# Norm factors along the rows: column sums by a product with ones, the root by Ln, Exp and one Newton step

## The chip, the cores and the metric

The kernel runs on one core of one Trainium2 chip. The metric is the device time of one execution in microseconds (us); the time before is the median of three runs.

## The reference, cut to what matters

One input of 512 tokens with 1024 features goes through three layers, all in float32. The first layer mixes three branches (gated linear attention, sliding-window attention, pooling) and has a feed-forward network with a short convolution; the second has attention with a forget gate ("fox") and a feed-forward network; the third has attention over a latent ("MLA") and a feed-forward network. Between all of them stand norms over the features of a token:

```python
def rmsnorm(x, gain):
    xf = x.astype(jnp.float32)
    var = jnp.mean(xf * xf, axis=-1, keepdims=True)
    return (xf * lax.rsqrt(var + RMS_EPS) * gain.astype(jnp.float32)).astype(x.dtype)
# first_block:  x = x + rmsnorm(merged @ w_out, norm_mix_post);  x = x + rmsnorm(f, norm_ffn_post)
# every layer:  h = rmsnorm(x, ...) ahead of each projection;  the last: rmsnorm_2(x, final_norm)
```

What concerns the change is the factor `1 / sqrt(mean of squares + eps)`, one number for each of the 512 tokens.

## The kernel before, in words

All activations are held transposed: the features lie in the 128 partitions (eight tiles of 128 features, `xk(0)` to `xk(7)`), the 512 tokens along the rows. A matmul with a weight tile gives 128 output features by 512 tokens in one PSUM bank. Each float32 product is made of three fp32r matmuls (`mm3`, high and low parts), so TensorE (PE) has some 10,500 matmuls. The weights come in 360 chunks of eight 128x128 tiles in the order of `tfk_plan`; each chunk is loaded by SP, cast to its high part by ScalarE (ACT, L277) and gets its low part from VectorE (DVE, L278), two chunks ahead of use (`take`, `_split`).

The order on PE is written out: the program runs `proj` calls in sequence, and small generators ("tasks") are stepped between them by `tick` when a modelled PE clock has passed their due time, which the constants `LAG` set. The order on the other engines comes from a scheduler with priorities, and each engine runs its instructions in that order, waiting for what is not ready.

A norm factor is needed along the rows, in all partitions, since it multiplies tiles of features by tokens. The squares are added over the eight tiles in `acc` (128x512), by GpSimd (POOL) and for the last tile by DVE (L507). Then:

- `tok_sums` multiplies each 128 tokens of `acc` with one column of ones: the sums come out by token, one number in each partition, and there are four pairs of weight load and matmul for 512 tokens, each in two passes.
- `_rsqrt` makes the root on DVE of these few numbers: an estimate from the bits and three Newton steps, some 12 tiny instructions.
- `bcast` puts the factors on a diagonal (DVE, L490) and multiplies it with ones on PE, so that they stand along the rows in a PSUM bank (`bc`); `stats_task` copies it to SBUF (L518) as `rsb`.

Who uses this: `stats` (task `stats_task`), for the norms ahead of projections, eight times: `mix_pre`, `ffn_pre`, `fox_norm`, `ffn_a`, `kv_in`, the two latents of MLA (`dkv`, `dq`), `ffn_b`; `chain` in `post_norm`, for the two norms behind the mixer (`wout`) and the first feed-forward network (`down0`), each in two halves of 256 tokens; `finish`, the last norm, in two halves, at the very end. `mix_pre` and `fox_norm` also need the factor by token (`rst`), since there values are projected with tokens in the partitions. In `chain` each half is followed by eight products on DVE (L962), eight additions to x on POOL (L963) and the splitting of x for the next projection (`x_ready`: L420 on ACT, L421 on DVE, the squares L504, L507), while PE is at the second half of the projection or at the first half of the next layer. In `finish` eight products (L1007) are followed by the stores of the output.

Of the kernel before, what the change touches and what calls it, by code (L numbers as in the profile page):

```python
# [7 lines left out]
F32 = mybir.dt.float32  # L8
F32R = mybir.dt.float32r
I32 = mybir.dt.int32  # L10
AF = mybir.ActivationFunctionType
# [184 lines left out]
class Net:  # L196
    def __init__(self, ctx, tc, xin, wall, par, cst, msk, nar, out, dbg=None):
# [15 lines left out]
        self.ones = self.cpool.tile([P, P], F32, name="ones")  # L213
        nc.gpsimd.memset(self.ones, 1.0)
        self.lows = [self.cpool.tile([P, 2, T], F32R, name=f"lows{i}") for i in range(2)]
        self.ident = self.c("ident", 128)
# [267 lines left out]
    def bcast(self, rs):  # L484
# [10 lines left out]
        return pb  # L495

    def tok_sums(self, acc, out, ms=range(4)):
        for i, m in enumerate(ms):
            self.mm(out[:, i:i + 1], acc[:, m * P:(m + 1) * P], self.ones[:, 0:1], True, True)
# [9 lines left out]

    def stats_task(self, acc, d, fut, lag):  # L510
        nc = self.nc
        pt = self.ps("tok")
        self.tok_sums(acc, pt)
        rs = self.rsqrt(pt[:, 0:4], 1.0 / d, 4)
        yield LAG[lag]
        pb = self.bcast(rs)
        rsb = self.pool.tile([P, T], F32, tag="rsb", name="rsb", bufs=2)
        nc.scalar.copy(out=rsb, in_=pb)  # L518
        fut.set((rsb, rs))

    def stats(self, acc, d, lag="sums", lag2="rsqrt"):
        fut = Fut(self)
        self.tasks.insert(0, [self.stats_task(acc, d, fut, lag2), self.clock + LAG[lag]])
        return fut
# [9 lines left out]
    def x_ready(self, k, cols=ALL):  # L534
# [20 lines left out]
        if self.next_gain == "final":  # L555
            nc.scalar.activation(out=x, in_=x, func=AF.Copy, scale=self.p("final", k))
        elif k == 7 and cols != HALVES[0]:
            self.rs = self.stats(self.acc, 1024, "sums_first" if self.next_gain == "mix_pre" else "sums" if cols == ALL else "sums_late")

# [376 lines left out]
    def post_norm(self, name, xs, gain, nxt, group, whole):  # L936
# [15 lines left out]
        def chain(h):  # L952
            cols = HALVES[h]
            pt = self.ps("tok")
            self.tok_sums(acc, pt, (2 * h, 2 * h + 1))
            rs = self.rsqrt(pt[:, 0:2], 1.0 / 1024, 2)
            yield LAG["chain"]
            pb = self.bcast(rs)
            for t in range(8):
                yt = y[t // 2][:, t % 2, cols]  # L960
                x = self.xk(t)[:, cols]
                v.tensor_tensor(out=yt, in0=yt, in1=pb[:, 0:256], op=ALU.mult)  # L962
                nc.gpsimd.tensor_tensor(out=x, in0=x, in1=yt, op=ALU.add)  # L963
                self.x_ready(t, cols)

        self.x_start(nxt)
# [6 lines left out]
    def residual(self, name, xs, nxt, k0=0, group=0):  # L973
# [3 lines left out]
        for t in range(8):  # L977
            x = self.xk(t)
            if nxt == "final" and t == 7:
                for h, cols in enumerate(HALVES):  # L980
                    ps = self.proj(name, t, xs, k0, None, cols)
                    with self.tc.high_priority(offset=2000):
# [3 lines left out]
                        self.nc.scalar.activation(out=x[:, cols], in_=x[:, cols], func=AF.Copy, scale=self.p("final", t))  # L986
                    self.tasks.insert(0, [self.finish(h, sq), self.clock + LAG["last"]])
                continue
# [5 lines left out]
    def finish(self, h, sq):  # L994

        nc, v = self.nc, self.nc.vector
        cols = HALVES[h]
        pt = self.ps("tok")
        for i, m in enumerate((2 * h, 2 * h + 1)):
            for a in (self.acc, sq):  # L1000
                self.mm(pt[:, i:i + 1], a[:, m * P:(m + 1) * P], self.ones[:, 0:1], a is self.acc, a is sq)
        rs = self.rsqrt(pt[:, 0:2], 1.0 / 1024, 2)
        yield LAG["last_rsqrt"]
        pb = self.bcast(rs)
        for k in range(8):
            x = self.xk(k)[:, cols]
            v.tensor_tensor(out=x, in0=x, in1=pb[:, 0:256], op=ALU.mult)  # L1007
            if k % 2:
                nc.sync.dma_start(out=self.out[:, k - 1:k + 1, cols], in_=self.x[k // 2][:, :, cols])
# [420 lines left out]
```

## Time and profile before

| | us |
|---|---|
| median of three runs | 2225.93 (2223.95 to 2228.35) |
| the profiled execution, its own time | 2225.05 |
| its span in the trace | 2223.3 |
| PE busy | 2165.1 (97%) |
| DVE busy | 1423.7 (64%) |
| ACT busy | 1022.2 (46%) |
| POOL busy | 282.1 (13%) |
| mean granted PE clock | 0.991 |

The span is what the trace covers; the profiled execution's own time is 1.75 us longer. "Busy" counts the time in which an engine has at least one instruction under way. A row of a timeline gives start, duration, engine, line, operation, tiles, and in brackets how long the engine had been idle before it and what ended that.

### The profile page before, as it was taken

The numbers are of one execution on the slowest core, as the hardware profiler recorded it, in microseconds if no ns is written. First come the engines' busy times: TensorE is split into PE (matmuls) and PEld (weight loads), VectorE is DVE, ScalarE is ACT, GpSimd is POOL, SyncE is SP. The second block draws the span as 40 slices with busy tenths as digits, with TensorE's granted clock in tenths as the row PEclk, the third lists the DMA queues.
The fourth block names the chain that finished last, engine by engine and source line by source line (L and its number), as shares of the span: only waits on it lengthen the run. The fifth ranks groups of instructions, "written<-read, shape, count | busy, mean of one in ns | idle before, by whom it ended". The sixth has DMA issues, their size and how long they took to land.

```text
span 2223.3 us, 27520 instructions
## 1 busy us (share of the span) xinstructions
PE 2165.1 (97%) x10536; PEld 1822.0 (82%) x10536; DVE 1423.7 (64%) x2372; ACT 1022.2 (46%) x1676; POOL 282.1 (13%) x242
## 2 busy tenths in 40 slices
PE   8989999999999998999999999999999999999998
PEld 6777788898888897888888888887888888888887
DVE  6897545578777238787677774357646567777524
ACT  4454232445444235676544443245755655444322
POOL 5221000040000004464200000102100101000010
PEclk9999999999999999999999999999999999999999
DMA  4211333322233344433233323332122223333332
GB/s 163 76 39 48 95 95 95 114 89 73 96 101 97 95 126 133 134 105 97 84 93 97 95 95 98 101 100 76 48 76 67 67 60 98 99 95 95 96 103 96
DMA packets 61956, 206.29 MB, mean 93 GB/s; under 512 B 7152, under 2 KB 9584, under 8 KB 61824
## 3 DMA queue, kind: packets, MB, share of 16 engines
q1 hardware_dynamic: 61392, 203.74, 29.4%
q8 instruction: 83, 1.36, 0.2%
q10 hardware_dynamic: 432, 0.79, 0.1%
q14 instruction: 49, 0.40, 0.1%
HBM read 197.65 MB, written 2.13 MB: 90 GB/s over the span
## 4 chain that ended last, share of the span: by engine, by line
PE 84%; DVE 9%; ACT 3%; issue 2%; DMA 1%; POOL 0%; SPq 0%; DVEq 0%; ACTq 0%; POOLq 0%
PE up L340 32%; PE down L340 15%; PE mout L340 4%; PE uq L340 3%; PE sc L340 2%; PE gate_a L340 2%; PE gate_b L340 2%; PE gate_c L340 2%; PE wout L340 2%; PE fout L340 2%; DVE lo L278 2%; DVE xs L421 1%; PE mpo L340 1%; PE dq L340 1%; PE fq L340 1%
## 5 line engine op out<-in xcount | busy, mean ns | idle before, releaser
L278 DVE TENSOR_TENSOR lo<-raw,hi 128x1024 fp32r<-128x1024 f32 (+1 forms) x348 | 438.1, 1259 | 318.0 <-ACT hi L277 313.6
L340 PE MATMUL up<-xs,hi 128*128 128x512 f32 x2016 | 621.8, 390 | 0.0
L277 ACT CAST hi<-raw 128x1024 fp32r<-128x1024 f32 (+1 forms) x348 | 365.2, 1049 | 554.2 <-PE down L340 170.5
L340 PEld LDWEIGHTS up<-xs,hi 128*128 128x128 f32 x2016 | 378.3, 188 | 78.9 <-issue 1.0
L340 PE MATMUL up<-xs,lo 128*128 128x512 f32 x1008 | 392.2, 389 | 0.0
L340 PE MATMUL down<-hl,hi 128*128 128x512 f32 (+1 forms) x1188 | 332.6, 366 | 0.0
L340 PEld LDWEIGHTS down<-hl,hi 128*128 128x128 f32 x1188 | 214.9, 189 | 36.2
L340 PEld LDWEIGHTS up<-xs,lo 128*128 128x128 f32 x1008 | 189.3, 188 | 39.6
L340 PE MATMUL down<-hl,lo 128*128 128x512 f32 (+1 forms) x594 | 217.1, 365 | 0.0
L507 POOL TENSOR_TENSOR acc<-acc,sq 128x256 f32<-128x256 f32 (+1 forms) x48 | 56.1, 1169 | 765.2 <-ACT sq L504 763.6
L1024 DVE TENSOR_TENSOR u<-up,rsb 128x512 f32<-128x512 f32 x132 | 90.1, 685 | 80.9 <-PE up L340 76.7
L1026 ACT ACTIVATE c<-u,par 128x512 f32<-128x512 f32 x132 | 107.0, 814 | 59.9 <-DVE u L1024 59.8
L340 PEld LDWEIGHTS down<-hl,lo 128*128 128x128 f32 x594 | 112.0, 189 | 18.0
L1027 DVE SCALAR_TENSOR_TENSOR c<-u,par,c 128x511 f32<-128x511 f32 x132 | 98.3, 746 | 23.8 <-ACT c L1026 23.7
L963 POOL TENSOR_TENSOR x<-x,yo 128x256 f32<-128x256 f32 x32 | 28.6, 930 | 633.3 <-DVE yo L962 633.3
L1028 DVE SCALAR_TENSOR_TENSOR c<-u,par,c 128x510 f32<-128x510 f32 x132 | 98.8, 749 | 4.0
L340 PE MATMUL uq<-hl,hi 128*128 128x512 f32 x288 | 89.5, 391 | 1.4 <-POOL hl L458 1.4
L457 ACT CAST hl<-c 128x512 fp32r<-128x512 f32 x66 | 40.7, 617 | 104.6 <-DVE c L1035 104.6
L340 PE MATMUL mout<-hl,hi 128*128 128x512 f32 x256 | 79.9, 393 | 0.0
L1033 ACT ACTIVATE c<-c 128x512 f32<-128x512 f32 x66 | 41.6, 630 | 70.4 <-DVE c L1028 70.3
L421 DVE SCALAR_TENSOR_TENSOR xs<-x,par,xs 128x512 fp32r<-128x512 f32 (+1 forms) x64 | 61.9, 1005 | 8.0 <-ACT xs L420 8.0
L340 PEld LDWEIGHTS uq<-hl,hi 128*128 128x128 f32 x288 | 53.9, 188 | 13.3 <-POOL hl L458 1.8
(398 smaller groups left out, 3933.9 us busy)
## 6 DMA issues: line engine op xcount, KB each, us to landing
raw<-in_wall_dram SPq DMA_DIRECT2D x359, 512.0 KB, 3.5
K<-KH SPq DMA_DIRECT2D x36, 128.0 KB, 2.3
bias<-cumd SPq DMA_DIRECT2D x16, 256.0 KB, 4.1
out_dram<-x SPq DMA_DIRECT2D x8, 256.0 KB, 2.3
x<-in_x_dram SPq DMA_DIRECT2D x7, 256.0 KB, 6.0
raw<-in_wall_dram SPq DMA_DIRECT2D x2, 256.0 KB, 3.9
early<-in_cst_dram SPq DMA_DIRECT2D x1, 512.0 KB, 6.5
msk<-in_msk_dram SPq DMA_DIRECT2D x1, 512.0 KB, 6.6
```

Source lines behind the costliest of these rows:

```text
L277: nc.scalar.copy(out=hi[:, c], in_=raw[:, c])
L278: nc.vector.tensor_tensor(out=lo[:, c], in0=raw[:, c], in1=hi[:, c].bitcast(F32), op=ALU.subtract)
L340: self.nc.tensor.matmul(out, lhsT=a, rhs=b, start=start, stop=stop)
L421: nc.vector.scalar_tensor_tensor(out=lo, in0=src, scalar=scale, in1=hi.bitcast(F32), op0=ALU.mult, op1=ALU.subtract)
L457: nc.scalar.copy(out=hi, in_=src)
L507: (eng or self.nc.vector).tensor_tensor(out=acc[:, cols], in0=acc[:, cols], in1=sq[:, cols], op=ALU.add)
L963: nc.gpsimd.tensor_tensor(out=x, in0=x, in1=yt, op=ALU.add)
L1024: v.tensor_tensor(out=u, in0=ps, in1=rsb, op=ALU.mult)
L1026: nc.scalar.activation(out=c, in_=u, func=AF.Identity, scale=self.p(conv, 88 + t), bias=self.p(conv, 132 + t))
L1027: v.scalar_tensor_tensor(out=c[:, 1:], in0=u[:, 0:T - 1], scalar=self.p(conv, 44 + t), in1=c[:, 1:], op0=ALU.mult, op1=ALU.add)
L1028: v.scalar_tensor_tensor(out=c[:, 2:], in0=u[:, 0:T - 2], scalar=self.p(conv, t), in1=c[:, 2:], op0=ALU.mult, op1=ALU.add)
L1033: nc.scalar.activation(out=g, in_=g, func=func)
```

## The change

The factors are now made along the rows. `all_sums` multiplies the whole 128x128 tile of ones with `acc`, so that each partition gets the sums of all tokens at once, in a PSUM bank. `row_factors` makes the root there, on 128x512 (or 128x256) elements: y = Exp(-0.5 Ln(s/d + eps)) on ACT, then one Newton step y (1.5 - 0.5 (s/d + eps) y^2), whose square is made on ACT and the rest on DVE. `stats` has a new argument `by_token`: `mix_pre` and `fox_norm` keep the old way; the six others, the four halves of `chain` and the two of `finish` take the new one. `stats_task` then has no second stage: the waiting time `rsqrt` and the product of `bcast` fall away. In `finish` the sum over `acc` is started at once and the last square added to it later.

```diff
+    def row_factors(self, sums, inv_d, out):
+        nc, v = self.nc, self.nc.vector
+        n = sums.shape[-1]
+        a, y, t = (self.t2(name=f"f{i}")[:, 0:n] for i in "ayt")
+        with self.tc.high_priority(offset=1000):
+            nc.scalar.activation(out=y, in_=sums, func=AF.Ln, scale=inv_d, bias=self.eps)
+            v.tensor_scalar(out=a, in0=sums, scalar1=-0.5 * inv_d, scalar2=-0.5 * EPS, op0=ALU.mult, op1=ALU.add)
+            nc.scalar.activation(out=y, in_=y, func=AF.Exp, scale=-0.5)
+            nc.scalar.activation(out=t, in_=y, func=AF.Square)
+            v.tensor_tensor(out=t, in0=a, in1=t, op=ALU.mult)
+            v.scalar_tensor_tensor(out=out, in0=t, scalar=1.5, in1=y, op0=ALU.add, op1=ALU.mult)
+        return out
+    def all_sums(self, accs, cols):
+        pt = self.ps("all")
+        n = cols.stop - cols.start
+        for i, a in enumerate(accs):
+            self.mm(pt[:, 0:n], self.ones, a[:, cols], i == 0, i == len(accs) - 1)
+        return pt[:, 0:n]
-    def stats_task(self, acc, d, fut, lag):
+    def stats_task(self, acc, d, fut, lag, by_token):
         nc = self.nc
+        if not by_token:
+            rsb = self.pool.tile([P, T], F32, tag="rsb", name="rsb", bufs=2)
+            fut.set((self.row_factors(self.all_sums([acc], ALL), 1.0 / d, rsb), None))
+            return
...
         def chain(h):
             cols = HALVES[h]
-            pt = self.ps("tok")
-            self.tok_sums(acc, pt, (2 * h, 2 * h + 1))
-            rs = self.rsqrt(pt[:, 0:2], 1.0 / 1024, 2)
-            yield LAG["chain"]
-            pb = self.bcast(rs)
+            rs = self.row_factors(self.all_sums([acc], cols), 1.0 / 1024, self.t2(name="rh")[:, 0:256])
             for t in range(8):
...
-                v.tensor_tensor(out=yt, in0=yt, in1=pb[:, 0:256], op=ALU.mult)
+                v.tensor_tensor(out=yt, in0=yt, in1=rs, op=ALU.mult)
...
-                    self.tasks.insert(0, [self.finish(h, sq), self.clock + LAG["last"]])
+                    self.tasks.insert(0, [self.finish(h, sq), self.clock])
...
-        pt = self.ps("tok")
-        for i, m in enumerate((2 * h, 2 * h + 1)):
-            for a in (self.acc, sq):
-                self.mm(pt[:, i:i + 1], a[:, m * P:(m + 1) * P], self.ones[:, 0:1], a is self.acc, a is sq)
-        rs = self.rsqrt(pt[:, 0:2], 1.0 / 1024, 2)
-        yield LAG["last_rsqrt"]
-        pb = self.bcast(rs)
+        pt = self.ps("all")[:, 0:256]
+        self.mm(pt, self.ones, self.acc[:, cols], True, False)
+        yield LAG["last"]
+        self.mm(pt, self.ones, sq[:, cols], False, True)
+        rs = self.row_factors(pt, 1.0 / 1024, self.t2(name="rh")[:, 0:256])
         for k in range(8):
             x = self.xk(k)[:, cols]
-            v.tensor_tensor(out=x, in0=x, in1=pb[:, 0:256], op=ALU.mult)
+            v.tensor_tensor(out=x, in0=x, in1=rs, op=ALU.mult)
```

## Rows read from the trace of the kernel before

**Rows 1.** The page: busy us, share of the span and instructions of each engine.

```profile
PE 2165.1 (97%) x10536; PEld 1822.0 (82%) x10536; DVE 1423.7 (64%) x2372; ACT 1022.2 (46%) x1676; POOL 282.1 (13%) x242
```

**Rows 2.** Waits of PE: total us, times, longest.

```profile
PE tok L340 <- DVE acc L507: 7.9, 4, 4.7
...
PE bc L340 <- DVE diag L490: 4.1, 3, 2.8
...
PE uq L340 <- POOL hl L458: 1.4, 1, 1.4
...
PE fv L340 <- DVE xs L421: 1.3, 2, 0.7
```

**Rows 3.** Timeline of PE at the token sums of `ffn_a`: start, us, operation.

```profile
1109.22 0.39 PE L340 MATMUL up<-xs,lo 128*128 128x512 f32 x1
1109.45 0.94 PE L340 MATMUL tok<-ones,acc 128*128 128x1 f32 x8
1110.26 0.72 PE L340 MATMUL up<-xs,hi 128*128 128x512 f32 x2
1110.82 0.40 PE L340 MATMUL up<-xs,lo 128*128 128x512 f32 x1
```

**Rows 4.** The same view at the broadcast product of `ffn_pre`.

```profile
506.13 1.02 PE L340 MATMUL bc<-diag,ones 128*128 128x512 f32 x2
506.59 0.80 PE L340 MATMUL up<-xs,khi 128*128 128x256 f32 x2
507.23 0.28 PE L340 MATMUL up<-xs,klo 128*128 128x256 f32 x1
```

**Rows 5.** Groups of ACT by line and shape: us in total, mean ns, idle before.

```profile
L1049 ACT ACTIVATE pb<-sc,nm 128x256 f32<-128x256 f32 x16 | 7.4, 463 | 0.0
...
L571 ACT ACT_TABLE_LOAD x3 | 3.8, 1283 | 1.1 <-DVE lc L570 1.1
L573 ACT ACT_TABLE_LOAD x3 | 3.8, 1283 | 0.1
```

**Rows 6.** Timeline of ACT in fox, where the function changes.

```profile
887.61 0.72 ACT L568 ACTIVATE le<-fz,par 16x512 f32<-16x512 f32 x1 [1.27 <-DVE fz L1104]
888.35 1.28 ACT L569 ACT_TABLE_LOAD   x1
```

**Rows 7.** Timeline of the end, both halves of `finish`.

```profile
2208.40 2.73 DVE L1007 TENSOR_TENSOR x<-x,bc 128x256 f32<-128x256 f32 x8 [1.14 <-PE bc L340]
...
2211.05 0.41 DVE L983 TENSOR_TENSOR x<-down,x 128x256 f32<-128x256 f32 x1
2211.50 0.42 ACT L985 ACTIVATE sq<-x 128x256 f32<-128x256 f32 x1 [9.43 <-DVE x L983]
...
2215.88 1.22 PE L340 MATMUL bc<-diag,ones 128*128 128x256 f32 x2 [2.79 <-DVE diag L490]
2217.13 2.73 DVE L1007 TENSOR_TENSOR x<-x,bc 128x256 f32<-128x256 f32 x8 [1.31 <-PE bc L340]
```

**Rows 8.** Timeline from `down0` into fox: first half of `chain`, sums of the second.

```profile
826.16 0.50 PE L340 MATMUL tok<-ones,acc 128*128 128x1 f32 x4
...
834.78 2.73 DVE L962 TENSOR_TENSOR yo<-yo,bc 128x256 f32<-128x256 f32 x8
...
838.79 0.28 PE L340 MATMUL down<-hl,lo 128*128 128x256 f32 x1
...
847.84 0.94 DVE L507 TENSOR_TENSOR acc<-acc,sq 128x256 f32<-128x256 f32 x1
```

**Rows 9.** Windows: length, busy us of PE, PEld, DVE, ACT, POOL; granted clock, DMA.

```profile
850.00:855.00 5.00, 5.00 (x15) 3.92 (x15) 4.57 (x16) 0.05 (x1) 0.00 (x0) 0.61 0.38 115
```

**Rows 10.** Timeline from `wout` into the first feed-forward network: sums of the second half.

```profile
474.70 0.79 PE L340 MATMUL tok<-ones,acc 128*128 128x1 f32 x4 [2.57 <-DVE acc L507]
```

**Rows 11.** The page's group of the weight casts, and their window up to 826.6 us.

```profile
L277 ACT CAST hi<-raw 128x1024 fp32r<-128x1024 f32 (+1 forms) x348 | 365.2, 1049 | 554.2 <-PE down L340 170.5
...
0.00:826.60 826.60, 144.51 (x139) 0.99 0.30 93
```

More of the change, by code (lines that the diff above doesn't have):

```diff
@@ L214, in __init__ @@
         nc.gpsimd.memset(self.ones, 1.0)
+        self.eps = self.cpool.tile([P, 1], F32, name="eps")
+        nc.gpsimd.memset(self.eps, EPS)
         self.lows = [self.cpool.tile([P, 2, T], F32R, name=f"lows{i}") for i in range(2)]
@@ L519, in stats_task, with stats @@
         fut.set((rsb, rs))
-    def stats(self, acc, d, lag="sums", lag2="rsqrt"):
+    def stats(self, acc, d, lag="sums", lag2="rsqrt", by_token=False):
         fut = Fut(self)
-        self.tasks.insert(0, [self.stats_task(acc, d, fut, lag2), self.clock + LAG[lag]])
+        self.tasks.insert(0, [self.stats_task(acc, d, fut, lag2, by_token), self.clock + LAG[lag]])
         return fut
@@ L557, in x_ready @@
         elif k == 7 and cols != HALVES[0]:
-            self.rs = self.stats(self.acc, 1024, "sums_first" if self.next_gain == "mix_pre" else "sums" if cols == ALL else "sums_late")
+            self.rs = self.stats(self.acc, 1024, "sums_first" if self.next_gain == "mix_pre" else "sums" if cols == ALL else "sums_late",
+                                 by_token=self.next_gain in ("mix_pre", "fox_norm"))
     def normed(self, gain):
@@ L961, in chain @@
                 x = self.xk(t)[:, cols]
-                v.tensor_tensor(out=yt, in0=yt, in1=pb[:, 0:256], op=ALU.mult)
+                v.tensor_tensor(out=yt, in0=yt, in1=rs, op=ALU.mult)
                 nc.gpsimd.tensor_tensor(out=x, in0=x, in1=yt, op=ALU.add)
                 self.x_ready(t, cols)
+            return
+            yield
         self.x_start(nxt)
```

## The prediction

> **What bounds the kernel now.** I read the page first: PE is busy for 97% of the span, DVE for 64%, ACT for 46% [rows 1]. So the time is PE's written-out order plus the places where PE stops. Next the waits of PE: 7.9 us in four waits of the token sums for `acc`, 4.1 us in three waits of the broadcast product for the diagonal, 1.4 us of MLA's queries, 1.3 us of fox's values [rows 2]. These are the waits that the change touches; none is in the middle of a feed-forward network. Then the timelines at each place where a factor is made, and the clock.
>
> **PE's stream.** The four pairs of the token sums of 512 tokens cost PE more than their records say. The next pair of fp32r matmuls starts 0.81 us behind them, and takes 0.56 us up to the third one where two such matmuls take 2 x 0.23 = 0.46: 0.92 us in all [rows 3]. The 128x512 float32 product of the broadcast costs 0.46 us up to the next start and 0.64 where a pair of 256 columns takes 0.24 (half of the 512 columns' 0.23 each [rows 3]): 0.86 us [rows 4]. The new sums have the same shape (128x128 ones against 128x512 float32), so I cost them at 0.86 too. Six of the eight `stats` go from 0.92 + 0.86 to 0.86: 6 x 0.92 = 5.5 us. Four halves of `chain` have half the columns and two of the four pairs: 4 x 0.46 = 1.8 us. Together **-7.3 us**, in stretches where PE never waits otherwise, so all of it is on the path. `finish` is in the tail below.
>
> **The new factor's latency.** On ACT: Ln reads PSUM with a bias tile; the nearest row is 0.46 us for 256 columns [rows 5]. Exp and Square are like L985's square, 0.42 [rows 7]. Ln and Exp each had a table load of 1.28 us ahead of them at all three places where the kernel had Ln and then Exp, and the load waited with the instruction for DVE [rows 5]; so I put two loads on the path of each factor, 2.57 us, not hidden by the wait for the sums. ACT: 2.57 + 0.46 + 0.42 + 0.42 = 3.9 us. DVE: two instructions of 0.41 (L983's length [rows 7]); the `tensor_scalar` runs beside ACT. Gaps between engines are 0.04 (2211.46 to 2211.50 [rows 7]), so three of them 0.1. A half takes **4.8 us** from the sums to the first product. Twelve factors add 24 loads; fox's first Exp and MLA's then find their table there, so ACT gets some 22 x 1.28 = 28 us more. ACT is at 46% [rows 1], which hides this by itself; what matters is who stands behind a load.
>
> For the six `stats` I take no cost from the latency. The old way had the waiting time `rsqrt` of 6.9 us in the order of PE, then 0.86, then a copy. The new one is at most 0.86 + 2.57 + 2 x (0.46 + 0.42 + 0.42 + 0.82) = 7.7 us, doubling the 256-column times for 512. So `rsb` comes no later, and PE goes on filling further banks meanwhile. If that cover is gone PE would stop for the difference, at most 2.6 us each if another 2.6 us of work stood ahead on ACT.
>
> **From `down0` into fox.** This is where PE stops longest: its sums for the second half were due behind the first values, and waited 4.7 us for `acc` (847.84 [rows 8], [rows 2]). DVE was at the eight splits of the first half's x before that addition, and those started from the first half's products at 834.78, 8.6 us behind the sums at 826.16 [rows 8]. After PE had stood idle up to 848.8 the granted clock was 0.61 of full for 5 us [rows 9], a mix of its two levels of 2.4 and 1.2 GHz: a loss of 5 x 0.39 = 2 us. In the new order the sums are there at about 826.16 + 0.6, and the products start 4.8 us later at 831.6, or 832.6 if a weight cast of 1.05 us [rows 11] stands ahead on ACT. That is 2.2 to 3.2 us earlier; POOL's additions, the splits and the addition to `acc` follow. The wait shrinks from 4.7 to about 2, with it goes some of the dip, and the two waits of fv for x (1.3 us) go because the second half gains the same latency. What is late next is POOL, which paces x at one addition per tile, and the token factor of `fox_norm`, unchanged. Bounds: 0 (DVE's order puts the splits first again, and the wait stays) and 4.7 + 2 + 1.3 = 8.0. I take **-5.0**, nearer to the row's shift of 2 to 3 us plus dip and fv waits.
>
> **From `wout` into the first network.** One wait of 2.57 us for `acc` [rows 10], same cause. Here the diagonal was ready early and the order of PE held it back, so the shift is 1 to 2 us. Bounds 0 and -2.6; **-1.5**.
>
> **MLA.** `dq`'s factor ends in the wait of 1.4 us for the queries and one of the three waits for the diagonal [rows 2]; of these 4.1 us the longest, 2.8, is in the tail, which leaves at most 1.3 here. The diagonal's wait cannot occur any more; the query wait shrinks if the factor comes earlier. Against it: ACT is shared with the rotary copies. Bounds -2.7 and +2.6 (both loads exposed); **-1.5**.
>
> **The tail.** Nothing hides it. First half: before, DVE's products began at 2208.40 and ran 2.73 us, and held the last addition of the projection (L983) until 2211.05 [rows 7]. In the new order the square's sums come about where the token sums were (`last` 2.8 us, now counted from behind the `acc` product: about 2204.7), so the products start at 2204.7 + 4.8 = 2209.5. The order on DVE is made by a scheduler; I expect about seven products ahead of L983, which PE's end would allow by 2209.5: L983 at 2209.5 + 7 x 0.34 = 2211.9, against 2211.05, +0.85. If L983 comes first it is at 2209.5, -1.5. Second half: from L983 to the first product were 6.08 us (2211.05 to 2217.13 [rows 7]). Now: 0.41 + 0.42 + sums on a PE that has just stood idle, 1.22 as for the broadcast there [rows 7], + 4.8 + 0.1 = 6.95: +0.85. Eight products and stores as before. Tail **+1.6**, bounds -0.7 (L983 first) and +2.9 (all eight products ahead, and a copy of x on ACT ahead of Ln).
>
> Of the table loads the Trainium skill, ScalarE: Activation LUTs, section What ACT_TABLE_LOAD costs, says that a switch costs 1283 ns and a drain of about 1380 ns. The length agrees. Of the drain the trace shows nothing: Abs ended at 888.33, the load began at 888.35 [rows 6].
>
> **Sum.** -7.3 - 5.0 - 1.5 - 1.5 + 1.6 = -13.7 us. Against the profiled execution's own 2225.05 that is **2211.4 us** (0.9 us under the median of the three runs, 2225.93, which I leave as it is).
>
> **The rivals.**
>
> *B. The waits stay.* DVE's order keeps splits ahead of the addition to `acc`, and the loads on ACT eat the gain in latency. Only stream and tail count: 2225.05 - 7.3 + 1.6 = 2219.4. For it: that wait comes from DVE's order, not from the factor's latency alone. Against: everything behind the products hangs on their start.
>
> *C. Slower: table loads in front of the weights.* ACT casts each weight chunk (L277), and a DVE product of `row_factors` that waits for ACT holds L278 behind it. Place: the second half of `down0`, where weights are used at 24 x 0.12 = 2.9 us a chunk. By 826.6 there had been 139 casts [rows 11], chunk 0 in two, so this one was chunk 137. By the plan `down0` ends at 138.4 chunks, at 838.9 [rows 8], so chunk 137 was needed at about 834.9: 8.4 us from cast to use, 6 less the cast and the low part. The mechanism decides once ACT and DVE together hold a cast for over 6 us; one factor holds them 4.8. If it did so at every factor, and nothing hid the loads: 12 x 2.57 = 30.8; 2225.05 - 7.3 + 30.8 = 2248.6.
>
> *D. One table for both functions.* If Ln and Exp came from one table, each factor would be 1.28 us shorter. Only the tail's two factors are wholly on the path: 2211.4 - 1.28 for the second half, and as much if the first half still holds L983: 2208.8. Against it: six loads at three Ln/Exp pairs [rows 5]. The Trainium skill, same page, section Table sets: the hidden batching unit, says that Ln and then Exp take one load, because a set holds both; this trace does not do so.
>
> *E. A switch costs more than its record*: 1.38 us for each of the tail's four loads at most, 2211.4 + 5.5 = 2216.9. Against it the gap of 0.02 us [rows 6]. This is the drain of the page named above.
>
> **How the numbers follow.** Forecast 0.57, B 0.22, C 0.11, D 0.06, E 0.04. The forecast's own bounds: with all terms at their good ends -7.3 - 8.0 - 2.6 - 2.7 - 0.7 = -21.3, 2203.8; B at its end is 2219.4 + 1.3 (tail) = 2220.7. The range is 2203.5 to 2221.0 and leaves out C and the outer part of B and MLA's loss. A measurement of this kernel can tell about 0.2% (4.5 us) from no change, so faster means below 2221.5: the forecast, D, E and most of B, 0.82; the rest of B and mild forms of C, 0.08; slower 0.10.
>
> **What would show it.** PE: token sums fall from 96 matmul records to 16; waits of the sums for `acc` fall to 2 to 5 us. ACT busy rises to about 1065 us, with two loads in each factor; wrong if a load hides behind the wait for the sums. Fox: the first products 4.8 to 6 us behind the sums. Tail: 6.9 us from L983 to the first product of the second half, L983 behind products of the first. Wrong, above all, if PE waits for low weight parts (L278) or for x appear that were not there, or if DVE stands at a product of `row_factors` while ready work waits behind it.

## The result and the profile after

| | before | after |
|---|---|---|
| median, us (four runs each) | 2225.22 (2223.95 to 2228.35) | 2250.36 (2248.01 to 2252.18) |
| ratio, with its 95% interval | | 1.0114 [1.0097, 1.0131] |
| span in the trace, us | 2223.3 | 2250.0 |
| mean granted PE clock | 0.991 | 0.985 |

The changed kernel is slower by 25.1 us, 1.1%. The forecast was 2211.4, faster.

First the busy times: for each engine us, share of the span, instructions. From the page of the kernel after:

```profile
PE 2163.4 (96%) x10460; PEld 1820.5 (81%) x10460; DVE 1425.5 (63%) x2252; ACT 1068.0 (47%) x1728; POOL 282.5 (13%) x243
```

Against [rows 1] PE has a little less to do and DVE 120 instructions fewer; ACT has 45.8 us more, as forecast ("about 1065"). No engine's busy time explains 25 us. They are PE's waits (us in total, times, longest), here those of the kernel after that the change touches:

```profile
PE all L342 <- DVE acc L531: 10.6, 2, 6.7
PE uv L342 <- DVE hl L460: 10.4, 1, 10.4
...
PE fq L342 <- DVE klo L280: 6.0, 1, 6.0
PE down L342 <- DVE lo L280: 5.1, 1, 5.1
...
PE tok L342 <- DVE acc L531: 2.7, 1, 2.7
```

The token sums waited 7.9 us for `acc` in [rows 2]; now the sums of both kinds (`all`, `tok`) wait 13.3. Three waits are new: MLA's `uv` for its split input, `down` and `fq` for the low part of a weight chunk (L280, which was L278).

Where the time went by stage. I took from each trace the start of the same instruction at the ends of six stages and subtracted the kernel before. The change touches nothing ahead of the first product of `wout`, so what the first column shows, up to 1.8 us, is scatter between executions.

| us longer than before | up to `wout` | to the first network (508.3) | to fox's first `fk` (906.2) | to the last `dq` (1509.0) | to the last `uv` (1762.9) | to the last `down` (2209.5) | to the end (2223.3) | whole span |
|---|---|---|---|---|---|---|---|---|
| after | 0.6 | 10.3 | 9.0 | -2.0 | 9.1 | -1.4 | 1.1 | 26.7 |

Three stages lose 28.4 us: the two behind `chain` (`wout` into the first network, `down0` into fox) and MLA behind `dq`. The forecast had each of them as a gain. The two stages that hold only `stats` (the fourth and sixth columns; the sixth ends with the first sums of `finish`) gain, as forecast.

The work at `down0` into fox, DVE and ACT of the kernel after (start, us, engine, line, operation; in brackets the idle time before and what ended it):

```profile
838.02 1.23 DVE L280 TENSOR_TENSOR lo<-raw,hi 128x1024 fp32r<-128x1024 f32 x1 [1.72 <-ACT hi L279]
...
842.45 0.42 DVE L510 SCALAR_TENSOR_TENSOR rh<-ft,fy 128x256 f32<-128x256 f32 x1
842.91 5.98 DVE L987 TENSOR_TENSOR yo<-yo,rh 128x256 f32<-128x256 f32 x8
848.82 1.74 DVE L280 TENSOR_TENSOR lo<-raw,hi 128x1024 fp32r<-128x1024 f32 x1
...
870.31 5.98 DVE L987 TENSOR_TENSOR yo<-yo,rh 128x256 f32<-128x256 f32 x8
876.21 1.74 DVE L280 TENSOR_TENSOR klo<-raw,khi 128x1024 fp32r<-128x1024 f32 x1
```

```profile
838.01 1.28 ACT L505 ACT_TABLE_LOAD   x1
839.30 0.47 ACT L505 ACTIVATE fy<-all,eps 128x256 f32<-128x256 f32 x1
839.79 1.28 ACT L507 ACT_TABLE_LOAD   x1
841.09 0.42 ACT L507 ACTIVATE fy<-fy 128x256 f32<-128x256 f32 x1
841.54 0.42 ACT L508 ACTIVATE ft<-fy 128x256 f32<-128x256 f32 x1
841.86 1.03 ACT L279 CAST hi<-raw 128x1024 fp32r<-128x1024 f32 x1
```

and PE there, in the same kernel:

```profile
837.09 0.59 PE L342 MATMUL all<-acc,ones 128*128 128x256 f32 x2
...
845.07 0.40 PE L342 MATMUL down<-hl,hi 128*128 128x256 f32 x2
850.61 0.58 PE L342 MATMUL down<-hl,lo 128*128 128x256 f32 x1 [5.14 <-DVE lo L280]
...
862.49 0.59 PE L342 MATMUL all<-acc,ones 128*128 128x256 f32 x2
```

Three things stand in these rows. The chain of the factor is as forecast: products 842.91 - 837.09 = 5.8 us behind the start of the sums, where it was 8.6 [rows 8]. On ACT the cast of a weight chunk (841.86) has the whole factor with its two loads ahead of it. And on DVE the eight products take 5.98 us, where [rows 8] has 2.73, and the low part of that chunk, castable since 842.9, comes behind them at 848.82. PE, which needs it, stands for 5.1 us. The second half repeats this: its sums (862.49) no longer wait for `acc`, where they had waited 4.7 us [rows 2], but its products (870.31) take 5.98 us again, the low part `klo` comes behind them at 876.21, and `fq` stands 6.0 us for it. The first four experiments take the order, the length of the products and the loads one at a time; the rest put them together and go by place.

### The profile page after: what moved, and what is told of

It is laid out like the page before. It is cut to its first block, busy times and chain, and to the rows that moved or that the text cites. A ratio compares the mean times of both kernels' runs of the same rounds, so it can differ in the third digit from the quotient of the medians.

```text
span 2250.0 us, 27332 instructions
## 1 busy us (share of the span) xinstructions
PE 2163.4 (96%) x10460; PEld 1820.5 (81%) x10460; DVE 1425.5 (63%) x2252; ACT 1068.0 (47%) x1728; POOL 282.5 (13%) x243
## 4 chain that ended last, share of the span: by engine, by line
PE 84%; DVE 9%; ACT 4%; issue 2%; DMA 1%; POOL 0%; SPq 0%; DVEq 0%; ACTq 0%; POOLq 0%
PE up L342 31%; PE down L342 15%; PE mout L342 4%; PE uq L342 3%; PE sc L342 3%; PE gate_a L342 2%; PE gate_b L342 2%; PE gate_c L342 2%; PE fout L342 2%; PE dq L342 1%; PE fq L342 1%; PE fv L342 1%; PE wout L342 1%; PE fk L342 1%; DVE lo L280 1%
## 5 line engine op out<-in xcount | busy, mean ns | idle before, releaser
L280 DVE TENSOR_TENSOR lo<-raw,hi 128x1024 fp32r<-128x1024 f32 (+1 forms) x348 | 436.8, 1256 | 325.6 <-ACT hi L279 321.1
```

The lines of the kernel that those rows point to most:

```text
L280: nc.vector.tensor_tensor(out=lo[:, c], in0=raw[:, c], in1=hi[:, c].bitcast(F32), op=ALU.subtract)
```

## The experiments

Each edit is against the kernel after. My theories were three: *order* (the program now issues products, x and the next sums earlier than PE's modelled clock would have, so due times and DVE's order moved), *operand* (the eight products read both inputs from SBUF, beside POOL), and *loads* (24 table loads in front of weights and splits: rival C).

### One cause at a time

**Order in `chain`**: the waiting time `chain` is put back between the factor and its products.

```diff
             rs = self.row_factors(self.all_sums([acc], cols), 1.0 / 1024, self.t2(name="rh")[:, 0:256])
+            yield LAG["chain"]
             for t in range(8):
...
-            return
-            yield
```

> The changed kernel took 2250.4 us. Here only the place in the program changes: chain waits its old 5.9 us of modelled PE clock between the factor and the products, as before the change, so that the products, the additions and x_ready are emitted as late as they were. Theory O (order: without that wait everything that chain emits stands 5.9 us earlier in the order of DVE and ACT, ahead of weight splits, and the next sums are asked for 5.9 us earlier by PE): the waits of PE for sums (10.6 us) and for low weight parts (12.6 us) mostly go, 2232 to 2240 us; MLA's wait of 10.4 us stays. Theory P (DVE's products read the factor from SBUF and run at 0.82 us instead of 0.41 beside POOL) and theory L (24 table loads hold ACT): the time moves by under 4 us, 2246 to 2251 us.

Measured: 2241.78 us, ratio 1.0072 [1.0050, 1.0095]; 8.6 us of the loss are gone. That lies between the two ranges. PE's wait of `all` for `acc` fell from 10.6 to 4.3 us, but the waits for low weight parts did not go, as the theory had it: they are 13.6 us, at `fv` and `down`, where they were 12.6 at `fq`, `down` and `fv`.

**Order in `stats`**: the waiting time `rsqrt` is put back between the factor and its use.

```diff
-            fut.set((self.row_factors(self.all_sums([acc], ALL), 1.0 / d, rsb), None))
+            rs = self.row_factors(self.all_sums([acc], ALL), 1.0 / d, rsb)
+            yield LAG[lag]
+            fut.set((rs, None))
             return
```

> Only the six stats tasks change: each waits its old second lag (6.9 or 5.85 us of modelled PE clock) between factor and use, so that what depends on it is emitted as late as before the change. Theory O: MLA's wait of uv for hl (10.4 us) goes, the waits at chain stay: 2239 to 2245 us. Theory L: that wait comes from the 1.28 us loads ahead of the query latent's factor, which stay: 2248 to 2251 us.

Measured: 2243.47 us, 1.0082 [1.0053, 1.0112]; 6.9 us, in the range of the order. But the wait of `uv` did not go: 6.5 of its 10.4 us are left, and the stage of MLA gains 4.1 (table below). With two executions, 2242.20 and 2244.75 us, the total is rough.

**Operand**: the factor of `chain` is written to a PSUM bank, so that its eight products have one input in PSUM, as before.

```diff
-            rs = self.row_factors(self.all_sums([acc], cols), 1.0 / 1024, self.t2(name="rh")[:, 0:256])
+            rs = self.row_factors(self.all_sums([acc], cols), 1.0 / 1024, self.ps("fac")[:, 0:256])
```

> Only the place of the factor in chain changes: the last instruction of the root writes it to a PSUM bank, and the 32 products read it there as before the change. Theory P: the products come back to 0.41 us, 32 x 0.41 = 13 us less on DVE in front of the splits; the waits behind the two chains shrink by 8 to 13 us: 2237 to 2242 us. Theory O: the products are faster, yet the same instructions stand first: 2245 to 2250 us.

Measured: 2244.21 us, 1.0086 [1.0052, 1.0119]; 6.2 us, between the two ranges. The two executions are 5 us apart (2241.71 and 2246.71 us), so the size is rough; as a step between combinations, below, it is clear. The groups of DVE (total us, mean ns | idle before), first of the kernel after, where L987 is `chain` and L1032 `finish`:

```profile
L987 DVE TENSOR_TENSOR yo<-yo,rh 128x256 f32<-128x256 f32 x32 | 24.0, 820 | 0.1
...
L1032 DVE TENSOR_TENSOR x<-x,rh 128x256 f32<-128x256 f32 x16 | 5.5, 417 | 0.1
```

of the kernel before, whose line L962 is L987 now:

```profile
L962 DVE TENSOR_TENSOR yo<-yo,bc 128x256 f32<-128x256 f32 x32 | 10.9, 412 | 1.8 <-PE bc L340 1.8
```

and of the kernel with the factor in PSUM:

```profile
L987 DVE TENSOR_TENSOR yo<-yo,fac 128x256 f32<-128x256 f32 x32 | 10.9, 412 | 0.1
```

The same product of the same shape takes 820 ns on average with both inputs in SBUF while POOL adds to x, 417 with both inputs in SBUF in `finish`, where POOL stands, and 412 with one input in PSUM beside the same additions of POOL. So it is neither SBUF nor POOL alone but both together: shown, since only the place of one operand differs between L987 here and there. The Trainium skill, SBUF — State Buffer, section Who interferes with whom, states this as a rule: a DVE instruction with two SBUF inputs contends with a GpSimd instruction that reads SBUF, one with at most one SBUF input, outside the two-port modes, does not. The trace agrees, with 820 against 412 ns.

**Loads**: Ln and Exp are replaced by functions that need no load, and the scalars so that the factor is a constant (with these scalars it is (-0.5 + 1.5) x 1 = 1; the recorded expectations say 1.5, which changes no time); the nine norms that use the twelve new factors are left out of the computation. In the order of the program PE, DVE, POOL and SP have the same instructions as in the kernel after. ACT has 22 fewer: the 24 loads go, and two that the kernel before had at the first Exp of fox and of MLA come back.

```diff
-            nc.scalar.activation(out=y, in_=sums, func=AF.Ln, scale=inv_d, bias=self.eps)
-            v.tensor_scalar(out=a, in0=sums, scalar1=-0.5 * inv_d, scalar2=-0.5 * EPS, op0=ALU.mult, op1=ALU.add)
-            nc.scalar.activation(out=y, in_=y, func=AF.Exp, scale=-0.5)
+            nc.scalar.activation(out=y, in_=sums, func=AF.Identity, scale=0.0, bias=self.ones[:, 0:1])
+            v.tensor_scalar(out=a, in0=sums, scalar1=0.0, scalar2=-0.5, op0=ALU.mult, op1=ALU.add)
+            nc.scalar.activation(out=y, in_=y, func=AF.Copy, scale=1.0)
```

> The 24 table loads go: Ln and Exp are replaced by Identity and Copy, and the Newton step by one with constants, so that the factor is a constant 1.5 (the norms that use the new factor are left out); PE, DVE, POOL and SP have the same instructions in the same order as in the changed kernel, ACT too but for the loads. Theory L: up to 12 x 2.57 = 31 us come back: 2220 to 2230 us. Theories O and P: 2.6 to 5 us in the tail and part of MLA's wait: 2240 to 2247 us.

Measured: 2236.57 us, 1.0048 [1.0029, 1.0068]; 13.8 us, between the two ranges. The groups of ACT in the kernel after show what was taken away:

```profile
L505 ACT ACT_TABLE_LOAD x12 | 15.4, 1283 | 12.3 <-PE all L342 12.2
L507 ACT ACT_TABLE_LOAD x12 | 15.4, 1283 | 0.2
```

Of these 30.8 us of loads, less the 2.6 that came back, 13.8 were on the path. No single cause is the whole: each edit alone gives 6 to 14 us back, and the kernel stays slower than before with any one of them.

### The causes together

These are combinations of the edits above: both orders; both orders and PSUM; both orders, PSUM and no loads (with the constant factor, so the same norms are left out).

> The waits in the program's order of chain and of the six stats together (e1 gave 2241.8, e2 2243.5, the changed kernel 2250.4). If the two act at different places, their gains add: 8.6 + 6.9, so 2233 to 2238 us. If they act on one chain of work: 2239 to 2242 us.

> Both old orders, and chain's factor in PSUM, so that of the change only the way of the sums, the root (with its 24 table loads) and finish are left. Additive theory: e5 less the 6.2 us of e3: 2227 to 2232 us, and the waits for low weight parts behind chain go. If the products' speed is worth nothing once the order is the old one: as e5, 2233 to 2238 us.

> As e6, and without the table loads (Identity and Copy for Ln and Exp, a constant factor of 1.5; the norms with the new factor are left out). If order, the operand in SBUF and the loads are all of the loss, what stays is the gain in PE's stream that was forecast (7.3 us) and a tail without loads: 2211 to 2218 us. If there is a fourth cause: 2222 us or more.

| | median, us | ratio to before | step, us |
|---|---|---|---|
| after | 2250.36 | 1.0114 [1.0097, 1.0131] | |
| both orders | 2240.64 | 1.0071 [1.0048, 1.0094] | -9.7 |
| and PSUM | 2230.89 | 1.0026 [1.0015, 1.0038] | -9.8 |
| and no loads | 2217.98 | 0.9963 [0.9945, 0.9981] | -12.9 |

The last one is 7.2 us under the kernel before (2225.22): with the edits for the three causes, what is left comes near the forecast's own stream term of -7.3, though it also holds the MLA wait below and the shorter tail, so the nearness is partly luck. It is at the upper end of the expected range, and its five executions lie between 2214.28 and 2223.25. The two orders together give 9.7, in the range for one chain of work, and not the sum of 8.6 and 6.9. With PSUM the time is in the range of the sum, but the waits for low weight parts behind `chain` did not go, as that text expected: 9.8 us are left at `fv` and `down`, and 6.6 at `fv` without the loads too, where the kernel before had 1.0. Why they are left stays open. By stage:

| us longer than before | up to `wout` | first network | fox's `fk` | last `dq` | last `uv` | last `down` | end | span |
|---|---|---|---|---|---|---|---|---|
| after | 0.6 | 10.3 | 9.0 | -2.0 | 9.1 | -1.4 | 1.1 | 26.7 |
| order in `chain` | -1.3 | 3.1 | 9.3 | -2.9 | 8.8 | -1.4 | 1.1 | 16.7 |
| order in `stats` | -1.0 | 9.5 | 7.9 | -4.0 | 5.0 | -1.4 | 1.1 | 17.1 |
| PSUM | 0.5 | 6.0 | 7.5 | -1.2 | 9.1 | -1.4 | 1.1 | 21.6 |
| no loads | 0.3 | 5.7 | 5.1 | -1.3 | 5.8 | -1.4 | -2.7 | 11.5 |
| both orders | 1.8 | 2.6 | 8.6 | -2.8 | 5.5 | -1.4 | 1.1 | 15.4 |
| and PSUM | 0.0 | -0.7 | 3.7 | -2.9 | 5.4 | -1.4 | 1.2 | 5.3 |
| and no loads | 0.7 | -3.8 | -0.2 | -2.5 | 3.3 | -1.4 | -2.7 | -6.6 |

The stages have different causes. Into the first network the order in `chain` is worth 7 us, PSUM or the loads alone 4 to 5. In fox's stage the order alone does nothing (9.0, 9.3, 8.6): there PSUM gives 5 and the loads 4 on top of it. PSUM alone gives 1.5 there: the waits of `down` and `fq` shrink from 5.1 and 6.0 us to 1.7 and 1.4, but PE then waits 3.7 at `fv` and 5.8 instead of 2.7 for the token sums of `fox_norm`. In MLA only the order in `stats` and the loads count. The tail changes with the loads alone, by 3.8. Where the two orders gain, they add by stage: 7.2 and 4.1 alone, 7.7 and 3.6 together, into the first network and in MLA. What the second gained elsewhere is of the size of the first column's scatter and did not come again.

### One place at a time

**The due time of the next sums.** `sums_late` counts from the point where the program has x ready, and that point moved up by the 5.9 of `chain`. Only the constant is changed:

```diff
-    "sums_first": 19.0, "lat": 3.19, "lat_rsqrt": 5.85, "sums": 8.32, "sums_late": 13.0, "rsqrt": 6.9, "chain": 5.9, "keep": 3.5,
+    "sums_first": 19.0, "lat": 3.19, "lat_rsqrt": 5.85, "sums": 8.32, "sums_late": 18.9, "rsqrt": 6.9, "chain": 5.9, "keep": 3.5,
```

> The changed kernel (2250.4 us) with one constant: the sums ahead of the first network and of fox are due 18.9 us of modelled PE clock behind x, not 13.0, since without the wait in chain x is emitted 5.9 us earlier. If PE merely asks too early for sums that come when they come, the 6.7 us wait ahead of the first network goes and the time falls by 4 to 7 us: 2243 to 2246 us. If x itself is late, PE waits elsewhere: 2249 to 2252 us.

Measured: 2241.18 us, 1.0073 [1.0054, 1.0091], 9.2 us, more than expected. The stage into the first network goes from +10.3 to +1.8; 2.1 more come in fox's, where the wait of 2.7 us for the token sums is gone. PE of the kernel after, at the sums of `wout`'s second half and of `ffn_pre`:

```profile
476.85 1.22 PE L342 MATMUL all<-acc,ones 128*128 128x256 f32 x2 [3.93 <-DVE acc L531]
...
501.97 2.07 PE L342 MATMUL all<-acc,ones 128*128 128x512 f32 x2 [6.70 <-DVE acc L531]
```

and at the latter with the later due time:

```profile
501.39 1.12 PE L342 MATMUL all<-acc,ones 128*128 128x512 f32 x2 [0.28 <-DVE acc L531]
```

`acc` is finished at nearly the same time in both, 502.0 and 501.4. PE asked for it 6.7 us early, stood, and then had the same products of the network still to do; with the later due time it does them in the meantime. The wait of 3.9 stays. `acc` itself was late too: the same place in the kernel before, with PSUM and with no loads, in this order:

```profile
498.74 0.61 PE L340 MATMUL tok<-ones,acc 128*128 128x1 f32 x4 [0.18 <-DVE acc L507]
...
498.27 2.07 PE L342 MATMUL all<-acc,ones 128*128 128x512 f32 x2 [7.94 <-DVE acc L531]
...
497.53 2.08 PE L342 MATMUL all<-acc,ones 128*128 128x512 f32 x2 [6.70 <-DVE acc L531]
```

The new factor was to bring `acc` forward, and it came some 3 us later than before. With PSUM and with no loads PE still stands as long or longer, but for an `acc` that comes 3.7 and 4.4 us earlier, which is most of what these two edits gain in this stage (4.3 and 4.6). Part of the stage's loss was the clock behind such waits. Windows from `wout`'s sums on, of the kernel after (length, busy us of PE, PEld, DVE, ACT, POOL; granted clock, DMA share, GB/s):

```profile
450.00:522.00 72.00, 60.78 (x450) 58.48 (x449) 45.87 (x63) 38.58 (x71) 25.29 (x28) 0.91 0.19 63
```

and of the kernel before:

```profile
450.00:522.00 72.00, 69.25 (x509) 66.29 (x508) 55.29 (x109) 34.24 (x67) 24.10 (x28) 0.98 0.22 65
```

PE is busy for 8.5 us less in the same stretch, and the clock is at 0.91 of full instead of 0.98; 59 matmuls fewer are done by its end.

**`chain` as before**, with the new `stats` and `finish`:

```diff
-            rs = self.row_factors(self.all_sums([acc], cols), 1.0 / 1024, self.t2(name="rh")[:, 0:256])
+            pt = self.ps("tok")
+            self.tok_sums(acc, pt, (2 * h, 2 * h + 1))
+            rs = self.rsqrt(pt[:, 0:2], 1.0 / 1024, 2)
+            yield LAG["chain"]
+            pb = self.bcast(rs)
...
-                v.tensor_tensor(out=yt, in0=yt, in1=rs, op=ALU.mult)
+                v.tensor_tensor(out=yt, in0=yt, in1=pb[:, 0:256], op=ALU.mult)
...
-            return
-            yield
```

> chain is wholly as before the change (token sums, root of two columns on DVE, diagonal, product in PSUM, its wait); the six stats and finish stay changed. If the two places behind chain are where the time goes, the 10.3 us up to the first network and the 11.7 us through fox come back, and MLA's 10.4 us of wait and 1 us of tail stay: 2227 to 2231 us. If stats (ffn_pre and the loads in it) cost there too: 2234 us or more.

Measured: 2231.07 us, 1.0027 [1.0015, 1.0038], at the upper end of the first range. By stage, in the columns from the first network on: -0.4, -0.9, -1.1, 8.7, -1.4, 1.1, span 6.0. Both chain stages are cured whole, by 10.7 and 9.9; MLA stays as it was. So nothing in fox's stage comes from `ffn_pre`, and nothing in MLA from `chain`.

**`dq` alone by token:**

```diff
-            return c, self.stats(acc, P * n, "lat", "lat_rsqrt")
+            return c, self.stats(acc, P * n, "lat", "lat_rsqrt", by_token=n == 6)
```

> The changed kernel (2250.4 us) with only the query latent dq as before the change (token sums, root on DVE, diagonal, product, copy). If MLA's wait of 10.4 us comes from this one factor (its early place in the order of DVE and its two loads), it goes: 2240 to 2243 us. If kv_in or dkv cause it: 2248 us or more.

Measured: 2243.13 us, 1.0081 [1.0063, 1.0100], at the upper end of the first range. The MLA stage goes from +9.1 to +0.1, and the wait of `uv` for the split is gone: the whole loss of that stage is one of the twelve factors. How, the rows of the kernel after at that place tell (DVE and ACT, from the factor of `dq` to the casts that `uv` waits for):

```profile
1537.73 0.67 DVE L510 SCALAR_TENSOR_TENSOR rsb<-ft,fy 128x512 f32<-128x512 f32 x1
1539.75 5.10 DVE L1220 SCALAR_TENSOR_TENSOR lat<-lat,par,rsb 128x512 f32<-128x512 f32 x6
...
1546.51 0.68 DVE L1233 TENSOR_TENSOR rr<-rr,sw 128x512 f32<-128x512 f32 x1
1547.22 0.62 ACT L459 CAST hl<-rr 128x512 fp32r<-128x512 f32 x1 [4.55 <-DVE rr L1233]
...
1550.98 0.58 ACT L459 CAST hl<-uk 128x512 fp32r<-128x512 f32 x1
```

On DVE the six products of the latent stand ahead of the rotary copy `rr`, so ACT waits 4.55 us for `rr`, and behind that cast stand those of the latent and of `uk`, whose banks PE needs. With the old, slower factor the latent was not ready so early in the program and `rr` and `uk` went first, as the kernel before shows:

```profile
1519.83 0.68 DVE L1208 TENSOR_TENSOR rr<-rr,sw 128x512 f32<-128x512 f32 x1
...
1521.19 1.08 ACT L457 CAST hl<-uk 128x512 fp32r<-128x512 f32 x2
...
1523.61 4.05 DVE L1195 SCALAR_TENSOR_TENSOR lat<-lat,par,rsb 128x512 f32<-128x512 f32 x6
```

The wait of `uv` is 10.4 us in the kernel after and 6.5 with the order in `stats`, where ACT's casts of `uk` stand ahead of the latent's. It is 4.0 in the kernel with both orders, PSUM and no loads. That these last 4.0 us come from the order of DVE, which is the same in all three, is argued from these rows only; the edits that I had for it left DVE's order as it is, so it was not tried by itself.

**What is left of use**: `chain`, `finish` and `dq` as before, the new factor only in `ffn_pre`, `ffn_a`, `kv_in`, `dkv` and `ffn_b`. The edit is the two last ones together, and in `finish`:

```diff
-                    self.tasks.insert(0, [self.finish(h, sq), self.clock])
+                    self.tasks.insert(0, [self.finish(h, sq), self.clock + LAG["last"]])
...
-        pt = self.ps("all")[:, 0:256]
-        self.mm(pt, self.ones, self.acc[:, cols], True, False)
-        yield LAG["last"]
-        self.mm(pt, self.ones, sq[:, cols], False, True)
-        rs = self.row_factors(pt, 1.0 / 1024, self.t2(name="rh")[:, 0:256])
+        pt = self.ps("tok")
+        for i, m in enumerate((2 * h, 2 * h + 1)):
+            for a in (self.acc, sq):
+                self.mm(pt[:, i:i + 1], a[:, m * P:(m + 1) * P], self.ones[:, 0:1], a is self.acc, a is sq)
+        rs = self.rsqrt(pt[:, 0:2], 1.0 / 1024, 2)
+        yield LAG["last_rsqrt"]
+        pb = self.bcast(rs)
...
-            v.tensor_tensor(out=x, in0=x, in1=rs, op=ALU.mult)
+            v.tensor_tensor(out=x, in0=x, in1=pb[:, 0:256], op=ALU.mult)
```

> Of the change only five factors are kept: ffn_pre, ffn_a, kv_in, the latent dkv and ffn_b; chain, finish and the query latent dq are as before the change. If the loss hangs only on the factors that something urgent waits for, PE's stream keeps 5 x 0.92 = 4.6 us and nothing else moves: 2219 to 2222.5 us, 0.2% faster than before. If loads or order cost at these five too: 2225 us or more.

Measured: 2222.03 us against 2224.17 of the kernel before, measured beside it, 0.9990 [0.9981, 0.9999]: 2.1 us faster, in the expected range. It is the only complete version that beats both kernels, by less than the 4.6 that five factors at 0.92 should give. PE's waits in it are those of [rows 2] again:

```profile
PE tok L342 <- DVE acc L531: 7.5, 3, 4.5
...
PE bc L342 <- DVE diag L492: 4.2, 3, 2.8
```

In its trace the step at the new sums from `ffn_a` on is there. Into the first network it is not: that stage is 0.7 us longer, at a granted clock of 0.96 where the kernel before has 0.98. From fox's first `fk` to its last it loses 2.5 us that no changed instruction accounts for. PE waits 2.15 us there for a transfer (`K<-KH`), where its longest such wait was 1.7 before, and behind it the granted clock is 0.61 and then 0.82 for 3 us each, where the whole stretch has 1.00 in the kernel before. The kernel after loses 2.7 in the same stretch, the one with the order in `chain` 0.1. Why nearly equal waits are followed by a lower clock in some traces only, no run shows.

## Why the prediction was wrong, point by point

**PE's stream: right.** Where a stage holds only a new `stats`, it is shorter by about 0.9 us per factor or a little more in nearly every kernel that has it (`ffn_a` -0.9, `kv_in` and `dkv` -2.4 together, `ffn_b` -0.9); forecast was 0.92. The first half of `finish` is shorter by 0.5, as forecast for a half of `chain` (0.46).

**The latency of a factor: right.** 5.8 us from the start of the sums to the first product in fox, forecast 4.8 to 6; two loads in each factor, 24 in all. That no load would hide was not so: in three of the twelve factors (`ffn_a`, `ffn_b` and the tail's first half, 2228.34 below) the first load ran ahead of the sums that Ln then waited for.

**The tail: right.** The timeline of the kernel after, both halves (ACT, PE and DVE):

```profile
2228.34 1.28 ACT L505 ACT_TABLE_LOAD   x1
2230.13 0.59 PE L342 MATMUL all<-sq,ones 128*128 128x256 f32 x2
2230.76 0.47 ACT L505 ACTIVATE fy<-all,eps 128x256 f32<-128x256 f32 x1 [1.13 <-PE all L342]
...
2234.50 2.77 DVE L1032 TENSOR_TENSOR x<-x,rh 128x256 f32<-128x256 f32 x8
2237.19 0.42 DVE L1010 TENSOR_TENSOR x<-down,x 128x256 f32<-128x256 f32 x1
...
2238.95 1.28 ACT L505 ACT_TABLE_LOAD   x1 [0.29 <-PE all L342]
...
2243.91 0.42 DVE L1032 TENSOR_TENSOR x<-x,rh 128x256 f32<-128x256 f32 x1
```

From L1010 to the first product 6.72 us, forecast 6.95. All eight products stand ahead of L1010, where I expected seven. The stage lost 1.1, with 0.5 of stream gained just before it: +0.6 net, forecast +1.6.

**From `down0` into fox and from `wout` into the first network: wrong, forecast -6.5, measured +19.3**, with the stream's gain there already in it. The waits that the terms were about went in fox (4.7 us for `acc`, 1.3 us of `fv` for x), and grew into the first network (2.6 to 3.9 and 0.2 to 6.7 us). In fox, waits for low weight parts took their place: 5.1, 6.0 and 1.5 us. Three steps failed.

The first is the sentence "In the new order the sums are there ... and the products start 4.8 us later", from which I let all that follows come earlier by the same time. The start came 2.8 us earlier against the sums; the eight products then took 5.98 us instead of 2.73, so the gain in latency was given back there. I had priced them as if nothing changed about them. But the same two lines of the diff that remove `pb` put the operand into SBUF, and rows of before already had the price: L278, which has two SBUF inputs, beside POOL's additions and away from them, on DVE before:

```profile
833.63 1.23 DVE L278 TENSOR_TENSOR lo<-raw,hi 128x1024 fp32r<-128x1024 f32 x1 [1.06 <-ACT hi L277]
...
837.43 1.83 DVE L278 TENSOR_TENSOR lo<-raw,hi 128x1024 fp32r<-128x1024 f32 x1
```

1.23 us alone, 1.83 beside POOL; and the addition to `acc` of 256 columns took 0.94 us in [rows 8], where POOL was adding at the same time, and 0.42 at 835.88 in the kernel after, where POOL stood. I read the row of 0.94 for its start and not for its length.

The second is that the waiting time `chain` was taken away as if it were only a time. It was also the point in the program behind which the products, x and the next due time stood. Moved up, the block passed the weight splits in the order of DVE, and PE asked for the next sums 5.9 us of its modelled clock earlier, when `acc` was not ready; no step of the sum looked at what the block had passed on DVE and ACT, nor at `sums_late`. Bound 0 for the good of the wait ("DVE's order puts the splits first again") was given, but no bound on the other side, where a block that comes first holds the splits.

The third is the loads, which the sum has only in the latency of a factor. "ACT is at 46% [rows 1], which hides this by itself; what matters is who stands behind a load" sees this, but whoever stands behind got no term in the sum, and a bound in MLA only. Without the loads the stage into the first network is 4.6 us shorter, fox's 3.9.

**MLA: wrong, forecast -1.5, measured +9.1**, outside the bound of +2.6. The step "both loads exposed" was the worst that I allowed; the loads are worth 3.3 there (9.1 to 5.8). The rest is again order, shown for 4.1 us (9.1 to 5.0 with the order in `stats`) and else argued: a factor that is ready early in the program pulls its six products ahead of the rotary copy and the casts that PE's banks wait for. "Against it: ACT is shared with the rotary copies" named the neighbour but not the queue behind it.

**The rivals.** B (the waits of the sums stay) came true into the first network only, not at fox's second half, whose wait it meant; nothing in its 2219.4 makes the kernel slower. C, at 0.11, had the right sign and nearly the time (2248.6), though by half of the mechanism: PE's new waits for low weight parts at `down` and `fq` are its symptom, and without the loads 13.8 of the 25.1 come back, not the 30.8 that it added. The rest is order and operand, which no rival had, so the nearness of its time is luck. What I had gone by against C was 6 us of slack against 4.8 of one factor. In the rows of `down0` above, the low parts of two successive chunks began at 838.02 and 848.82, 10.8 us apart, where a chunk was used in 2.9: the block that held them was the factor and the eight products behind it, and these were twice as long. D (one table) did not occur: 24 loads. E (the drain) did not either, see below.

**What I wrote would show it wrong** was the right list: "if PE waits for low weight parts (L278) ... or if DVE stands at a product of `row_factors` while ready work waits behind it". The first is what the waits show. The second is close: DVE did not stand, it worked on the products while ready work stood behind them.

## What to carry to other kernels

When a change moves a value from PSUM to SBUF, look at every reader's second operand and at what GpSimd does at that time, and price it by a row of the same kind beside GpSimd. When a change removes a waiting time from a written-out order, list what stood behind it (work on each queue, and due times that count from there), for all of it moves up, and work that comes early on an in-order engine is late for whoever was passed. The new factor gained only its matmuls here, 7.3 us by the forecast's sum; the kernel came out 25.1 us slower, so what came with it cost some 32 us, an estimate from these two.

## What the runs showed of the hardware that was not expected

A float32 product of 128x256 with both inputs in SBUF took 820 ns on average beside POOL's additions, from 417 at its shortest, and 412 with one input in PSUM; POOL's own additions took 977 ns there and 930 before, so DVE bore nearly all of it.

A table load can run ahead of the wait of the instruction that it belongs to: in the tail's two halves one load (2228.34) ran before the sums that Ln waited for, the other (2238.95) waited with them for 0.29 us. The trace shows what goes with it. Of L505 of the kernel after, whose twelve Ln have a load each:

```profile
L505 ACTq EVENT_SEMAPHORE  x6: 17/17/17, 478.1 to 2238.9; - x6
```

Six of the twelve have an instruction of ACT's sequencer ahead of the load that does nothing but wait, here for PE, and the load runs behind it, as at 2238.95. The other six have none; among these are the three whose load ran ahead of the sums (`ffn_a`, `ffn_b`, 2228.34), and none of these six loads waited. Beyond its 1.28 us it took nothing, here as in [rows 6]. On ACT of the kernel after, in `wout`'s first half:

```profile
454.31 1.28 ACT L505 ACT_TABLE_LOAD   x1
455.61 0.47 ACT L505 ACTIVATE fy<-all,eps 128x256 f32<-128x256 f32 x1
456.10 1.28 ACT L507 ACT_TABLE_LOAD   x1
```

Ln ended at 456.08 and the next load began at 456.10.
